# The update of the samples' retention state moves into each head's retention

## The chip, the cores and the metric

The kernel runs on one core of a Trainium2 chip. The metric is the device time of one execution in microseconds (us). Engines in the text: PE (TensorE, matrix products; its weight loads are listed as PEld), DVE (VectorE), ACT (ScalarE), POOL (GpSimd) and SP (SyncE, which issues most loads).

## The reference, cut to what matters

One step of a one-layer decoder with a prompt group (512 tokens) and a sample group (8 sequences of 8 new tokens). The layer adds up three sub-layers: a mixer of 8 retention heads and 8 differential-attention heads, a cross-attention to memory tokens and a SwiGLU FFN, each with a norm before and after. For the samples each retention head starts from a given state, gives its output and hands back the new state. With one chunk of 8 tokens for each sample:

```
scores = jnp.einsum('bihd,bjhd->bhij', qb, kb) * intra[None]
o = jnp.einsum('bhij,bjhv->bihv', scores, vb) + jnp.einsum('bihd,bhdv->bihv', qb, s) * q_dec
s_new = s * chunk_dec + jnp.einsum('bjhd,bjhv->bhdv', kb * k_dec, vb)
```

The last line is what the change moves. It is an output of its own (`ret_sample`, in the kernel `rets`), and nothing later in the layer reads it.

## The kernel before, in words

All activations stand with features on the 128 partitions and 576 columns (512 prompt tokens, 64 sample tokens). The stages, in the order of time: the input projection; the attention stage (455 to about 992 us), a loop over 8 heads; the output projection, up to 1179 us; a first handover; the query projection with the memory tokens' norm; cross-attention and its output product w_xo, up to 1416 us; a second handover; the gate, up and down products, up to the end. A handover is a norm between two dense products: DVE or POOL adds the last squares into an accumulator (line 1059 or 1169), `bcast_rstd` (from line 173) sums it over the partitions with 12 small passes on PE (`rsb_pr`, L179), takes the root on ACT and the reciprocal on DVE, spreads the factor with products against ones (`rsb_ps`, L203) and copies it. Then `prep_b1` or `prep_b2` scale the tiles and add the residual (`ym`, L1225 and L1227, L1474 and L1218), and the first product of the next stage can start.

One turn of the attention loop does, for head h: `ret_dense` (the projections of q, k, v of the next retention head in half blocks, L118), `diff_prompt` (the differential attention of the prompt), `sample_unit` (that of one sample sequence, whose key and value pages POOL gathers, `ku` and `vu`), `ret_head` (the retention) and `ret_gate`. `ret_head` puts the samples' keys (scaled by the decay) and values into a small tile `kvs` (`kns` and `vns`, lines 884 to 888). Further down it loads the samples' state in two groups of four samples into a tile `s0` of 256 KB (L951, on SP's queue) and multiplies it by the queries (`ros`, L952 and L962). `s0` has one buffer, so the second group's load waits until the first group's products have read it; the trace calls it `s`.

The update of the state is not in that loop. `ret_head` stores `kvs` to a scratch in DRAM (`kvd`, L889). In the two handovers `load_kvs` (L1102) loads it back, two heads at a time, and `state_update` runs sixteen times, eight in each handover: it loads a group's state again (L1107), forms `vbd`, the values spread over four blocks with the other samples' rows at zero (`bdm` is a mask of 0 and 1; L1108, DVE), multiplies it by the keys (`ru`, L1114, PE, a float32 product in two passes of 512 columns), does `s0 = s0 * decay + ru` (L1115, DVE) and stores the result to `rets` (L1116, on ACT's queue). `filler` places three updates ahead of the norm, three inside it behind the request for the bank of `rsb_pr`, and two after it.

What sets the order: the program is written in this order, and a planner that simulates the engines' time orders each engine's instructions and gives out the buffers. On the chip every engine, and every queue of transfers' issues, works in the order that the planner fixed. PSUM has eight banks; in attention three of them have the tag "a" (`bank_a`: scores, transposes and results of `diff_prompt`), one is that of `ret_head` (`rbank`). The pools of the next stage take over the banks and the SBUF of a closed one, and wait for its last reader. `r512` is a tag of three buffers of 128 x 512, used by `ret_head`.

Of the kernel before, what the change touches and what calls it, by code (L numbers as in the profile page):

```python
# [48 lines left out]
def step_kernel(ctx: ExitStack, tc: tile.TileContext, a: dict, o: dict):  # L49
# [164 lines left out]
    def slot(i, name, dtype=F32):  # L214
        pool = ap_ if i < 32 else spool["s2"]
        return pool.tile([P, T], dtype, tag=SL[i], name=name)
# [10 lines left out]
    def opslot(op, st):  # L227
        return op * 8 + st
# [129 lines left out]
    with ExitStack() as pha:  # L358
# [3 lines left out]
        gd = dp.tile([8, P, T], F32, name="gd")  # L362
        rawd = dp.tile([7, P, T], F32, name="rawd")
        kdec = cA.tile([P, 16], F32, name="kdec")
        kvd = dp.tile([NS, 8, 2 * P], F32, name="kvd")
        ph1 = pha.enter_context(ExitStack())
        spool["s2"] = ph1.enter_context(tc.tile_pool(name="s2a", bufs=1))
        fa = ph1.enter_context(tc.tile_pool(name="fa", bufs=1))
# [133 lines left out]
        def bank_a(name):  # L502
            return paa.tile([P, 512], F32, tag="a", name=name)
# [30 lines left out]
        def r512(name):  # L534
            return tA.tile([P, 512], F32, tag="r512", name=name, bufs=3)

        def rsmall(name, w=2):
            return tA.tile([P, 8], F32, tag="smallr", name=name, bufs=2)[:, :w]
# [165 lines left out]
        def sample_unit(b):  # L704
# [117 lines left out]
            if b == NB - 1:  # L822
                for h in range(8):
                    S.dma_start(mixd[8 + h][:, TP:], msb[:, h, :])

        NGA = 5
        omd = dp.tile([7 - NGA, P, T], F32, name="omd")
        rot = [None, None]
# [40 lines left out]
        def ret_head(h, q, k, v):  # L869
# [16 lines left out]
            kns, vns = kvs[:, :P], kvs[:, P:]  # L886
            V.tensor_scalar(kns, pss[:NS, 0:P], kdec[:NS, 8 + h : 9 + h], None, ALU.mult)
            V.tensor_copy(vns, pss[:NS, P : 2 * P])
            S.dma_start(kvd[:, h, :], kvs)  # L889
            V.tensor_tensor(  # L890
                scz[:, :, 24:32],
                pss[:NS, 256:320].rearrange("p (b t) -> p b t", b=NB),
# [55 lines left out]
            for g in range(2):  # L948
                pg = pos[:, g * P : (g + 1) * P]
                s0 = tA.tile([P, 4, P], F32, tag="s0", name=f"s0_{h}_{g}", bufs=1)  # L950
                SY.dma_start(s0, a["state"][h][:, 4 * g : 4 * g + 4, :])  # L951
                TE.matmul(  # L952
                    pg,
                    scz[:, 4 * g : 4 * g + 4, :].rearrange("p b c -> p (b c)"),
                    vns,
                    start=True,
                    stop=False,
                    skip_group_check=True,
                )
                for j in range(4):  # L960
                    c0 = TP + 8 * (4 * g + j) - 24
                    TE.matmul(  # L962
                        pg[32 * j : 32 * j + 32],
                        qd[:, c0 : c0 + 32],
                        s0[:, j, :],
                        start=False,
                        stop=True,
                        skip_group_check=True,
                    )
            rs = rsmall(f"rs{h}", 2)  # L970
            for g in range(2):
                sq = tA.tile([P, P], F32, tag="ssqr", name=f"rsqs{h}_{g}", bufs=1)
# [121 lines left out]
            t = kept[k]  # L1094
        xr.append(t)

    bdm = cp.tile([NS, NB], F32, name="bdm")
    SY.dma_start(bdm, a["bdm"])

    def load_kvs(i, sl):  # L1100
        t = slot(sl, f"kvs{i}_{sl}")[:NS, :512].rearrange("p (h c) -> p h c", h=2)
        SY.dma_start(t, kvd[:, 2 * i : 2 * i + 2, :])  # L1102
        return t

    def state_update(i, s0, vbd, kv, pu):
        h, c = i // 2, i % 2
        SY.dma_start(s0, a["state"][h][:, 4 * c : 4 * c + 4, :].rearrange("p b v -> p (b v)"))  # L1107
        V.tensor_tensor(  # L1108
            vbd.rearrange("p (b v) -> p b v", b=4),
            kv[:, h % 2 : h % 2 + 1, P:].to_broadcast([NS, 4, P]),  # L1110
            bdm[:, 4 * c : 4 * c + 4].unsqueeze(2).to_broadcast([NS, 4, P]),
            ALU.mult,
        )
        TE.matmul(pu, kv[:, h % 2, :P], vbd, start=True, stop=True)  # L1114
        V.scalar_tensor_tensor(s0, s0, (1.0 - 2.0 ** (-5.0 - h)) ** 8, pu, ALU.mult, ALU.add)  # L1115
        S.dma_start(o["rets"][h][:, 4 * c : 4 * c + 4, :].rearrange("p b v -> p (b v)"), s0)  # L1116

    NBF = 8
    sui = iter(range(16))

    def filler(kvs, s0l, vbl, bk):
        def fill(n):
            for _ in range(n):
                i = next(sui)
                s0 = slot(s0l[i % len(s0l)], f"s0_{i}")[:, :512]
                vbd = slot(vbl[i % len(vbl)], f"vbd{i}")[:NS, :512]
                state_update(i, s0, vbd, kvs[i // 4], bk(f"ru{i}"))

        def wrapped(n):
            def f(name):  # L1130
                t = bk(name)
                if name.endswith("_pr"):
                    fill(n)
                return t

            return f

        return fill, wrapped

    fill, wrapped = filler(  # L1140
        {i: load_kvs(i, opslot(OBL, i)) for i in range(NBF // 4)},
        [opslot(OBL, st) for st in (2, 3, 4, 5)],
        [opslot(OBL, st) for st in (6, 7)],
        fb2,
    )
    fill(3)
    bcast_rstd(acc1, rsb, D, T, "rsb1", wrapped(3))
    fill(2)
    ph2.close()

    pctx = ctx.enter_context(ExitStack())
# [304 lines left out]
    def fbank(name):  # L1456
        return pf.tile([P, 512], F32, tag="f", name=name)

    fill, wrapped = filler(
        {i: load_kvs(i, opslot(OAH, 1 + i - NBF // 4)) for i in range(NBF // 4, 4)},  # L1460
        [opslot(OAL, st) for st in range(1, 6)],
        [opslot(OAH, 3), opslot(OAL, 0)],
        fbank,
    )
    fill(3)
    bcast_rstd(acc3, rsf, D, T, "rsb2", wrapped(3))
    fill(2)

    e2 = strassen_env(fp, fbank)

# [471 lines left out]
```

## Time and profile before

| | us |
|---|---|
| median of 3 runs (lowest, highest) | 2993.5 (2993.02, 2995.7) |
| profiled execution, span of its instructions | 2994.0 |
| PE busy in it | 2856.2 (95%) |
| DVE, ACT, POOL busy | 2244.7, 1325.6, 369.1 |

The profile is of one execution. It gives no separate time for the profiled execution beside its span; that span lies among the times of the three runs. "Busy" is the share of the span in which an engine had an instruction; matmuls are pipelined and their ends are modelled. A row of a timeline gives start, duration, engine, line and operation, the output and the inputs by tile name, how many instructions are merged, and in square brackets the engine's idle time before it with what ended it.

### The profile page before, as it was taken

The page shows a single profiled execution, that of the slowest core. Times are in us where ns is not written, and L with a number is a line of the kernel's source. Part 1 is how long each engine was busy: PE and PEld are TensorE (multiplying, and loading weights), DVE is VectorE, ACT ScalarE, POOL GpSimd, SP SyncE. Part 2 cuts the span into 40 slices and gives each one's busy share as a digit, 9 for nine tenths or more (in the row PEclk, how much of TensorE's full clock was granted, in tenths as well). Part 3 has the DMA queues.
Part 4 walks back from the last instruction along what each step waited for, and adds up shares of the span by engine and source line. Part 5 has one row for each costly group of instructions (what it writes and reads, how often), then busy time and mean ns, then how long its engine had stood idle before and what let it go on. Part 6 is the DMA issues. An engine that isn't in the chain of part 4 may idle for free.

```text
span 2994.0 us, 54633 instructions
## 1 busy us (share of the span) xinstructions
PE 2856.2 (95%) x22060; PEld 2728.2 (91%) x22060; DVE 2244.7 (75%) x3464; ACT 1325.6 (44%) x2177; POOL 369.1 (12%) x340
## 2 busy tenths in 40 slices
PE   7899999999999999799799999999999999999996
PEld 7899998887877998788699999999999999999995
DVE  8677777555555876853798888888887877888986
ACT  7333344443445653544554444444444435433441
POOL 4000003323232021603500000000000000000004
PEclk9999999999999999899799999999999999999998
DMA  4433336666665445853734444444444465465431
GB/s 164 140 120 127 120 126 229 233 211 227 225 207 177 160 135 203 237 181 120 190 113 148 151 125 154 145 131 150 140 134 146 141 234 201 176 210 207 173 120 64
DMA packets 205336, 493.63 MB, mean 165 GB/s; under 512 B 26099, under 2 KB 68083, under 8 KB 205084
## 3 DMA queue, kind: packets, MB, share of 16 engines
q1 hardware_dynamic: 123420, 334.14, 34.5%
q0 software_dynamic: 22464, 75.38, 8.1%
q10 hardware_dynamic: 59200, 80.63, 7.4%
q8 instruction: 173, 2.83, 0.4%
q14 instruction: 79, 0.65, 0.1%
HBM read 407.08 MB, written 85.61 MB: 165 GB/s over the span
## 4 chain that ended last, share of the span: by engine, by line
PE 76%; DMA 7%; DVE 7%; issue 6%; ACT 2%; POOL 1%; SPq 1%; DVEq 0%; ACTq 0%; POOLq 0%
PE dX L1648 8%; PE Yg L307 6%; PE Yu L307 6%; PE Yin L307 5%; PE Xg L307 4%; PE dZ L1648 4%; PE Zu L307 4%; PE Zg L307 4%; PE Xu L307 4%; PE Xin L307 3%; PE Zin L307 3%; PE dY L1648 2%; PE Ywo L307 2%; PE rk L118 2%; PE xo L118 2%
## 5 line engine op out<-in xcount | busy, mean ns | idle before, releaser
L1648 PE MATMUL dX<-fo,wd 128*128 128x288 f32 x1872 | 269.4, 295 | 2.5 <-ACT ysl L54 2.5
L1648 PEld LDWEIGHTS dX<-fo,wd 128*128 128x128 f32 x1872 | 255.6, 188 | 2.8 <-ACT ysl L54 2.8
L1768 POOL TENSOR_TENSOR fin<-fin,ysq 128x320 f32<-128x320 f32 (+1 forms) x10 | 8.4, 841 | 1444.4 <-ACT ysq L54 1444.4
L54 ACT ACTIVATE wd<-wr_d 128x512 fp32r<-128x512 f32 x156 | 97.7, 630 | 119.8 <-PE dX L1648 56.7
L1648 PE MATMUL dZ<-fo,wd 128*128 128x288 f32 x936 | 139.4, 295 | 0.0
L1648 PEld LDWEIGHTS dZ<-fo,wd 128*128 128x128 f32 x936 | 129.2, 188 | 0.3 <-ACT ysl L54 0.3
L106 DVE TENSOR_TENSOR wd<-wr_d,wd 128x512 fp32r<-128x512 f32 x156 | 106.4, 687 | 12.4 <-ACT wd L54 11.6
L695 POOL DMA_INDIRECT vu<-cv,idx x64 | 61.6, 963 | 168.5 <-PE ou L787 124.2
L54 ACT ACTIVATE wd<-d 128x512 fp32r<-128x512 f32 x78 | 48.9, 631 | 75.6 <-PE dZ L1648 40.4
L1648 PE MATMUL dY<-fo,wd 128*128 128x288 f32 x468 | 75.5, 295 | 0.0
L695 POOL DMA_INDIRECT ku<-ck,idx x64 | 63.5, 993 | 94.9 <-PE su L726 57.6
L307 PE MATMUL Xg<-op,wh_p1g 128*128 128x288 f32 x336 | 67.6, 296 | 0.0
L307 PE MATMUL Xu<-op,wh_p1u 128*128 128x288 f32 x336 | 67.6, 296 | 0.0
L1648 PEld LDWEIGHTS dY<-fo,wd 128*128 128x128 f32 x468 | 66.7, 188 | 0.0
L54 ACT ACT_TABLE_LOAD x45 | 57.7, 1283 | 18.0 <-PE rsb_pr L179 11.9
L328 DVE TENSOR_TENSOR w_s1g<-w_a21g,wr_a22g 128x1024 f32<-128x1024 f32 x21 | 25.7, 1225 | 48.3 <-DMA w_a21g<-w_gate 48.3
L106 DVE TENSOR_TENSOR wd<-d,wd 128x512 fp32r<-128x512 f32 x78 | 53.5, 689 | 9.8 <-ACT wd L54 9.2
L307 PEld LDWEIGHTS Xg<-op,wh_p1g 128*128 128x128 f32 x336 | 53.9, 188 | 0.0
L307 PEld LDWEIGHTS Xu<-op,wh_p1u 128*128 128x128 f32 x336 | 53.9, 188 | 0.0
L307 PE MATMUL Xin<-op,wh_p1in 128*128 128x288 f32 x256 | 51.7, 296 | 0.0
L307 PE MATMUL Yg<-oph,wh_p7g 128*128 128x288 f32 x168 | 50.2, 299 | 1.1 <-DVE u2g L333 1.1
L307 PE MATMUL Yu<-oph,wh_p4u 128*128 128x288 f32 x168 | 49.7, 296 | 1.5 <-DVE u3u L347 1.5
(1153 smaller groups left out, 11132.2 us busy)
## 6 DMA issues: line engine op xcount, KB each, us to landing
fo<-fo SPq DMA_DIRECT2D x140, 288.0 KB
wr_d<-w_down SPq DMA_DIRECT2D x39, 512.0 KB
d<-w_down SPq DMA_DIRECT2D x39, 512.0 KB
fo<-sh ACTq DMA_DIRECT2D x60, 288.0 KB
fo<-sl ACTq DMA_DIRECT2D x60, 288.0 KB
w_a21g<-w_gate SPq DMA_DIRECT2D x21, 512.0 KB
wr_a11g<-w_gate SPq DMA_DIRECT2D x21, 512.0 KB
wr_a22g<-w_gate SPq DMA_DIRECT2D x21, 512.0 KB
```

Of the source, the lines that this page charges most:

```text
L54: S.activation(out, in_, func, **kw)
L106: V.tensor_tensor(lo, src, hi.bitcast(F32), ALU.subtract)
L118: TE.matmul(po, ws, x[h][xi], start=start and i == 0, stop=stop and i == 2)
L307: TE.matmul(bk[:, :HN], w[wx][:, st, :], ops[op][st][xi], start=first and st == 0 and i == 0, stop=st == 7 and i == 2, skip_group_check=True,)
L328: V.tensor_tensor(s1, a21, a22, ALU.add)
L695: G.indirect_dma_start(t, None, src, bass.IndirectOffsetOnAxis(ap=idx[:, pg : pg + 1], axis=0))
L1648: TE.matmul(bk[:, :HN], w[wi][:, st, :], ops[e][st][xi], start=start and st == 0 and i == 0, stop=st == 3 and i == 2, skip_group_check=True,)
L1768: (V if j % 2 == 0 or j > 11 else G).tensor_tensor(ac[:, hs], ac[:, hs], sq, ALU.add)
```

## The change

The update moves into the loop over the groups in `ret_head`, behind the products that read the state. There it uses the `s0` that is loaded already and the keys and values that are still in `kvs`. `vbd` takes a buffer of `r512`, the product takes a bank of `bank_a`, the result goes into `s0` itself and from there to `rets`. The scratch `kvd`, its stores and loads, the second load of the state, `state_update`, `filler` and the slots that they used go away. The mask is loaded once, in the attention stage. The two calls of `bcast_rstd` take plain banks.

```diff
-            S.dma_start(kvd[:, h, :], kvs)
...
+        bdm = cA.tile([NS, NB], F32, name="bdm")
+        SY.dma_start(bdm, a["bdm"])
...
                 (in ret_head, for g in range(2), after the products of s0)
+                vbd = r512(f"vbd{h}_{g}")[:NS]
+                V.tensor_tensor(
+                    vbd.rearrange("p (b v) -> p b v", b=4),
+                    vns.unsqueeze(1).to_broadcast([NS, 4, P]),
+                    bdm[:, 4 * g : 4 * g + 4].unsqueeze(2).to_broadcast([NS, 4, P]),
+                    ALU.mult,
+                )
+                pu = bank_a(f"ru{h}_{g}")
+                TE.matmul(pu, kns, vbd, start=True, stop=True)
+                s0f = s0.rearrange("p b v -> p (b v)")
+                V.scalar_tensor_tensor(s0f, s0f, g8, pu, ALU.mult, ALU.add)
+                S.dma_start(o["rets"][h][:, 4 * g : 4 * g + 4, :], s0)
...
-    fill, wrapped = filler(
-        {i: load_kvs(i, opslot(OBL, i)) for i in range(NBF // 4)},
-        [opslot(OBL, st) for st in (2, 3, 4, 5)],
-        [opslot(OBL, st) for st in (6, 7)],
-        fb2,
-    )
-    fill(3)
-    bcast_rstd(acc1, rsb, D, T, "rsb1", wrapped(3))
-    fill(2)
+    bcast_rstd(acc1, rsb, D, T, "rsb1", fb2)
...
-    fill(3)
-    bcast_rstd(acc3, rsf, D, T, "rsb2", wrapped(3))
-    fill(2)
+    bcast_rstd(acc3, rsf, D, T, "rsb2", fbank)
```

## Rows read from the trace of the kernel before

**Rows 1.** The page's first part: each engine's busy time, share, instructions.
```profile
PE 2856.2 (95%) x22060; PEld 2728.2 (91%) x22060; DVE 2244.7 (75%) x3464; ACT 1325.6 (44%) x2177; POOL 369.1 (12%) x340
```
**Rows 2.** Windows: stretch, length, busy PE PEld DVE ACT POOL, clock, DMA share, GB/s.
```profile
1178.90:1200.70 21.80, 15.94 (x34) 6.74 (x33) 15.58 (x25) 7.09 (x13) 2.02 (x3) 0.61 0.90 325
1416.10:1441.30 25.20, 17.76 (x34) 7.14 (x33) 16.81 (x26) 6.39 (x11) 1.11 (x2) 0.57 0.50 154
...
455.00:992.00 537.00, 509.51 (x4742) 427.67 (x4740) 303.95 (x836) 241.96 (x597) 167.21 (x175) 0.98 0.62 211
```
**Rows 3.** Windows of 4 us in the handovers, the same columns.
```profile
1180.00:1184.00 4.00, 3.05 (x7) 0.65 (x5) 2.54 (x3) 3.92 (x6) 1.43 (x2) 0.98 0.92 324
...
1196.00:1200.00 4.00, 2.92 (x4) 0.67 (x2) 3.72 (x7) 1.35 (x3) 0.00 (x0) 0.50 0.58 203
...
1436.00:1440.00 4.00, 2.58 (x4) 0.49 (x2) 4.00 (x7) 1.13 (x2) 0.88 (x1) 0.50 0.17 66
```
**Rows 4.** Timeline of the first handover.
```profile
1178.91 3.02 PE L1114 MATMUL ru<-vbd,kvs 64*128 64x512 f32 x6
...
1180.61 1.40 POOL L1059 TENSOR_TENSOR acc<-acc,osq 128x576 f32<-128x576 f32 x1 [0.59 <-ACT osq L54]
...
1183.78 0.69 DVE L1115 SCALAR_TENSOR_TENSOR s<-s,ru 128x512 f32<-128x512 f32 x1 [1.22 <-DMA s<-state]
1184.38 0.75 DVE L1059 TENSOR_TENSOR acc<-acc,osq 128x576 f32<-128x576 f32 x1
...
1189.49 2.08 PE L179 MATMUL rsb_pr<-ones,acc 128*96 128x1 f32 x12
...
1197.25 0.69 DVE L1115 SCALAR_TENSOR_TENSOR s<-s,ru 128x512 f32<-128x512 f32 x1 [0.28 <-PE ru L1114]
...
1198.64 0.78 ACT L54 ACTIVATE h2h<-ym,gains 128x576 fp32r<-128x576 f32 x1 [3.94 <-DVE ym L1227]
...
1199.87 0.68 DVE L1115 SCALAR_TENSOR_TENSOR s<-s,ru 128x512 f32<-128x512 f32 x1
...
1200.69 1.30 PE L118 MATMUL xq<-h2h,wh_xq 128*128 128x288 f32 x4 [1.77 <-ACT mt L54]
```
**Rows 5.** Timeline of the second handover.
```profile
1418.11 0.75 DVE L1169 TENSOR_TENSOR acc<-acc,psq 128x576 f32<-128x576 f32 x1
...
1427.81 2.08 PE L179 MATMUL rsb_pr<-ones,acc 128*96 128x1 f32 x12
...
1437.49 0.68 DVE L1115 SCALAR_TENSOR_TENSOR s<-s,ru 128x512 f32<-128x512 f32 x1
1438.08 1.42 DVE L1218 TENSOR_TENSOR ym<-ym,xk 128x576 f32<-128x576 f32 x2
...
1441.27 0.61 PE L118 MATMUL gu0a<-op,wh_gu 128*128 128x288 f32 x1 [2.69 <-ACT op L54]
```
**Rows 6.** The update's tiles: durations in ns (lowest/median/highest), first and last start.
```profile
L1114 PE MATMUL ru<-vbd,kvs x32: 589/1054/1219, 1178.9 to 1437.5; 64*128 64x512 f32 x32
L1108 DVE TENSOR_TENSOR vbd<-kvs,bdm x16: 676/677/1632, 1176.6 to 1428.5; 64x512 f32<-64x512 f32 x16
...
L1115 DVE SCALAR_TENSOR_TENSOR s<-s,ru x16: 672/687/689, 1183.8 to 1439.4; 128x512 f32<-128x512 f32 x16
```
**Rows 7.** Chain of waits, attention and first handover: start, us, what.
```profile
649.79 4.64 DMA s<-state
...
1187.56 4.05 DMA o_rets<-s
```
**Rows 8.** Waits of PE and of SP's queue, attention stage: total us, times, longest.
```profile
PE ros L962 <- DMA s<-state: 1.7, 2, 1.1
...
SPq L951 <- PE ros L962: 43.5, 9, 16.6
```
**Rows 9.** Timeline of the query stage, DVE and POOL.
```profile
1249.67 12.37 DVE L109 SCALAR_TENSOR_TENSOR mhl<-mt,gains,mhl 128x256 fp32r<-128x256 f32 x1 [0.25 <-ACT mhl L54]
...
1259.41 0.99 POOL L1190 TENSOR_TENSOR macc<-macc,mt 128x256 f32<-128x256 f32 x1
```

More of the change, by code (lines that the diff above doesn't have):

```diff
@@ L364, in step_kernel @@
         kdec = cA.tile([P, 16], F32, name="kdec")
-        kvd = dp.tile([NS, 8, 2 * P], F32, name="kvd")
         ph1 = pha.enter_context(ExitStack())
@@ L1095, in step_kernel @@
         xr.append(t)
[L1097 to L1112, printed above, removed]
-        )
[L1114 to L1138, printed above, removed]
-    fill, wrapped = filler(
-        {i: load_kvs(i, opslot(OBL, i)) for i in range(NBF // 4)},
-        [opslot(OBL, st) for st in (2, 3, 4, 5)],
-        [opslot(OBL, st) for st in (6, 7)],
-        fb2,
-    )
-    fill(3)
-    bcast_rstd(acc1, rsb, D, T, "rsb1", wrapped(3))
-    fill(2)
+    bcast_rstd(acc1, rsb, D, T, "rsb1", fb2)
     ph2.close()
@@ L1457, in fbank @@
         return pf.tile([P, 512], F32, tag="f", name=name)
[L1459 to L1464, printed above, removed]
-    fill(3)
-    bcast_rstd(acc3, rsf, D, T, "rsb2", wrapped(3))
-    fill(2)
+    bcast_rstd(acc3, rsf, D, T, "rsb2", fbank)
     e2 = strassen_env(fp, fbank)
```

## Prediction

> **What bounds the kernel now.** I read the page's engine shares first: TensorE is busy for 95% of the span, and no other engine comes near [rows 1]. A mean over stages does not price a move between two stages, so the next view is the table of windows over the three stretches that the change touches [rows 2]: the attention stage (455 to 992 us), the handover from the output projection to the query projection (1178.9 to 1200.7) and the one from w_xo to the gate and up product (1416.1 to 1441.3). In the attention stage PE is busy for 509.5 of 537 us at a granted clock of 0.98, DVE for 304, POOL for 167: PE is the bound, with 27.5 us of gaps. In the handovers PE shows 15.9 of 21.8 us and 17.8 of 25.2 us, but the dense work stands still and the clock is about 0.6. What runs there is the update and two short products of the norm. The timeline of both [rows 4, 5] shows which of it the next stage waits for; the grouped view of the update's tiles [rows 6] prices it; the chain and the waits around the loads of the state [rows 7, 8] show what the update meets in attention.
>
> **What the handovers give back.** In the first one the sum of squares is finished by DVE's add at 1184.38. Its other operand was ready when POOL's add ended, at 1180.61 + 1.40 = 1182.0. DVE stood behind an update (1183.78) that waited for its state to land. Without updates the add ends at 1182.0 + 0.75 = 1182.8. The norm's column sums on PE started only at 1189.49, behind update products in PE's queue; now they can start at about 1182.9, which is 6.6 us earlier [rows 4]. From there to the first query product three more updates of s0 lie in DVE's queue. Two of them (one is at 1197.25) stand ahead of the first normalised tile: some 0.6 us each, 1.2. The first xq product (1200.69) starts 0.14 us after the third ends (1199.87 + 0.68 = 1200.55), although its operand was ready at 1198.64 + 0.78 = 1199.4: the PSUM banks of the closing pool are still being read. That is 1.2 more. First handover: 6.6 + 1.2 + 1.2 = 9.0 us.
>
> In the second one the last add ends at 1418.11 + 0.75 = 1418.9 and the column sums start at 1427.81, behind six updates: 8.9 us. One update (1437.49) sits ahead of the add at 1438.08 on DVE, which feeds the first gate product at 1441.27: 0.5. Together 9.4 us [rows 5]. The sum of both is 18.4 us. What is late next is the norm's own chain (sums, square root, broadcast, scaling), which stays as it is. The clock costs nothing extra: it had fallen to 0.50 of full speed in both handovers with the updates in them, and is 0.50 in the last slice before the dense work is back [rows 3], so the sums keep their 2.08 us. The first stretch also loses 8 loads and 8 stores of 256 KB, 4.2 MB, where the queues ran at 325 GB/s [rows 2]: 12.9 us of transfer, more than the 9.0 us by which the work moves forward, so the loads should not hold it back.
>
> **What attention pays.** Each head gets two updates: two multiplies (vbd), two float32 products (ru, two passes each), two updates of s0 on DVE and two stores on ACT's queue. It loses one store to kvd; the 4 kvd loads and 16 second loads of the state go from the later stages, as attention has the state in SBUF anyway. SP gets no new load there except the small mask, once.
>
> PE: three ru products, six passes, took 3.02 us [rows 4] while the clock was at 0.98 of full [rows 3], 1.0 us each; the median pass of 1.05 us [rows 6] is at half clock. 16 x 1.0 = 16 us, in the stage that PE bounds. Bounds: 8 us if half of it falls into the 27.5 us of gaps, 16 if none does. I take 16: most gaps are waits of PE's queue for a particular operand, and nothing can overtake there.
>
> DVE: 16 x (0.68 + 0.69) = 22 us [rows 6] on an engine that is busy for 304 of 537. Cover: its idle 233 us. It is in the softmax chains' queue too; I take 1 us (0 to 22).
>
> The buffer: s0 has one slot. Today the second load of a head waits only for the first group's ros products. In the new order it waits for the update of s0 (0.69) and for its store to land, 4.05 in the nearest row [rows 7]: 4.7 us later, for 8 heads. The first load of the next head waits likewise but has most of a head (some 60 us) to spare. In SP's queue the waiting load stands in front of weight loads of the half blocks and of the q, k, v and bias loads; SP already stands 43.5 us in that place [rows 8], and the weights have three slots, so a few more us there hardly reach PE. On ACT each store waits in order behind its DVE update; the exponentials and copies of the softmax queue behind it. The ru result holds one of the three "a" banks of PSUM until its state has landed, and diff_prompt takes its banks from the same three. From below: nothing, if half-block products fill the extra time as they mostly do now, 1.7 us of PE idle for that load in the whole stage [rows 8]. From above: 8 x 4.7 = 38 us. The nearest row is the 1.7 us in two waits, 0.9 us each, under a load of 4.64 us; the new round trip is twice as long. I take one such wait for each head, 8 us with ACT's and PSUM's share in it. Attention: 16 + 1 + 8 = 25 us.
>
> After the last head the output projection needs the PSUM banks and the SBUF of the stage. Gate blocks run on PE up to about 992 and cover a round trip of 9.4 us that starts near 969. I take 0.
>
> **Sum.** -18.4 + 25 = +6.6 us on the profiled execution, whose span is 2994.0 us; the runs' median is 2993.5 us, so the span may stand for the time. Forecast: 3000 us.
>
> The first handover's add and a vbd show one more thing: the 16 multiplies have a median of 677 ns and a longest of 1632 ns [rows 6], and POOL's add was running from 1180.61 to 1182.0. In attention POOL is busy for 31% of the stage [rows 2], in the handovers for 9 and 4%. If each vbd that meets a POOL instruction takes 1.63 instead of 0.68 us, that is 16 x 0.31 x 0.95 = 4.7 us more on DVE. The Trainium skill has a rule for it ("SBUF — State Buffer", section "Who interferes with whom"): VectorE with two SBUF inputs and GpSimd shut each other out of a shared pair of ports for a whole instruction. By that rule the page gathers that POOL starts would wait as well; the longest vbd agrees with it, the median does not contradict it.
>
> **Rivals.** (1) Faster. Two things could give some 10 us more. The updates' products may fall into PE's gaps and the round trip may be covered wholly: attention +8, total -10, 2984 us. Or the query stage gains more than its start: its PE stands idle around 1250 to 1262 behind a single DVE instruction of 12.37 us, during a run of POOL adds [rows 9]. The memory tiles take the slots that the updates leave, so half of POOL's 16 memory adds, about 1 us each, can move into the empty handover: -8 on top, 2992; both together 2976. For it: PE's small wait for the state. Against it: a PE queue that is nearly full.
> (2) Slower by more: the round trip through s0 is exposed. The place is the second group's ros, the price up to 4.7 us a head. It decides once PE has no half-block products placed between the two groups. At half exposure 19 instead of 8 us: +17.6, 3012; at full exposure 3030. For it: this load is on the chain of waits already at 649.79 [rows 7]. Against it: only two waits of PE now.
> (3) DVE and POOL shut each other out as above, with the gathers late by as much: +4.7 on the forecast, 3005. For it: one slow vbd. Against it: PE waits for DVE rarely in that stage.
> (4) The change doesn't do what it says: the handovers don't shorten, because another wait takes the place of PE's queue. With half of the 18.4 us back: +15.8, 3010. Against it: both sums were ready long before PE began.
>
> **How the numbers follow.** Chances: forecast 0.45, (1) 0.25, (2) 0.15, (3) 0.10, (4) 0.05. The forecast alone reaches from 2993 to 3007. The range takes (1) down to 2982 and (2) at half exposure with a few us more, up to 3016. This kernel's measurement tells about 0.2%, 6 us, from no change, so slower begins at 2999.5 and faster at 2987.5. Half of the forecast, all of (2) and (4) and most of (3) lie above: 0.49. Most of (1) lies below: 0.20. Between: 0.31.
>
> **What would show it.** Right: the column sums start 3 to 4 us after the last dense product in both handovers, and the stretches shrink from 21.8 and 25.2 us to about 13 and 16; ru passes of 0.4 to 0.5 us stand in attention, which is about 25 us longer; PE's waits there for s grow from 1.7 us to about 8. Wrong: attention longer by under 12 us, or by over 35; a first handover that is no shorter; or a query stage that loses or gains more than its start, above all at the long DVE instruction.

## The result: 37 us slower, and the loss is in attention

The changed kernel takes 3030.4 us (median of 4 runs, 3029.27 to 3032.37); the kernel before, run beside it, 2993.7 us (4 runs, 2993.02 to 2995.7). The ratio is 1.0117, 95% interval [1.0103, 1.0132]. The forecast was 3000 us in a range of 2982 to 3016: the time lies above the range.

The page of the profile after, its first part. The span is 3029.3 us, 35.3 more than before. PE is busy for 3.9 us more [rows 1], so 31 of the 35 us are idle time of PE:
```profile
PE 2860.1 (94%) x22060; PEld 2737.5 (90%) x22060; DVE 2240.4 (74%) x3464; ACT 1330.7 (44%) x2180; POOL 375.1 (12%) x340
```
Windows of the changed kernel over the attention stage and the two handovers, columns as in [rows 2]. The handover windows reach from the last dense product to the next stage's first:
```profile
455.00:1045.00 590.00, 539.63 (x4776) 443.18 (x4774) 319.32 (x871) 250.93 (x604) 169.70 (x175) 0.95 0.58 200
1232.75:1245.50 12.75, 4.37 (x17) 3.17 (x16) 5.39 (x9) 7.04 (x17) 7.67 (x9) 0.60 0.64 233
1458.60:1474.40 15.80, 4.35 (x17) 3.18 (x17) 8.52 (x14) 6.35 (x11) 1.70 (x2) 0.56 0.29 93
```
Against [rows 2] the attention stage is 53 us longer (590 for 537), the first handover 9.0 us shorter (12.8 for 21.8) and the second 9.4 (15.8 for 25.2). Both handovers shrank by what was forecast. The timeline of the changed kernel shows how (compare [rows 4, 5]):
```profile
1232.46 0.29 PE L307 MATMUL Zwo<-oph,wl_p3wo 128*128 128x288 f32 x1
...
1235.56 0.76 DVE L1071 TENSOR_TENSOR acc<-acc,osq 128x576 f32<-128x576 f32 x1 [2.31 <-POOL acc L1071]
1236.37 2.08 PE L179 MATMUL rsb_pr<-ones,acc 128*96 128x1 f32 x12 [3.62 <-DVE acc L1071]
...
1245.51 1.33 PE L118 MATMUL xq<-h2h,wh_xq 128*128 128x288 f32 x4 [3.40 <-ACT h2h L54]
...
1458.14 0.42 PE L118 MATMUL xo<-oh,wl_xo 128*128 128x288 f32 x2
1461.53 2.05 PE L179 MATMUL rsb_pr<-ones,acc 128*96 128x1 f32 x12 [2.97 <-ACT yx L54]
...
1474.39 0.61 PE L118 MATMUL gu0a<-op,wh_gu 128*128 128x288 f32 x1 [5.81 <-ACT op L54]
```
The column sums now start 3.6 and 3.0 us after the last dense product; before, they started 10.5 and 11.7 us after it. So the account, from the first and last dense products of the stages in both traces, is: attention +53.3, output projection +0.5, first handover -9.0, query and cross-attention stage -2.4, second handover -9.3, the rest +2.2. The sum is +35.3, which is the difference of the spans.

Now the attention stage. The timeline of the changed kernel, retention of head 0 from the first group's products (`ros`) to the first transpose of head 1 (`rkn`); below it the end of head 6:
```profile
488.90 0.65 PE L962 MATMUL ros<-s,qd 128*32 128x128 f32 x8
...
524.08 0.66 PE L617 MATMUL nt_d<-ident,on 128*128 128x128 f32 x4
...
526.53 1.98 PE L978 MATMUL ru<-vbd,kvs 64*128 64x512 f32 x4
528.73 0.69 DVE L980 SCALAR_TENSOR_TENSOR s<-s,ru 128x512 f32<-128x512 f32 x1 [4.68 <-PE ru L978]
...
529.45 0.34 ACTq L981 DMA_DIRECT2D o_rets<-s  x1
...
536.38 0.33 SPq L951 DMA_DIRECT2D s<-state  x1
...
545.52 0.43 PE L962 MATMUL ros<-s,qd 128*32 128x128 f32 x8
...
551.50 0.38 PE L997 MATMUL rot<-ident,rob 128*128 128x128 f32 x2
...
558.03 1.11 PE L877 MATMUL rkn<-ident,rk 128*128 128x128 f32 x4
...
980.49 0.38 PE L997 MATMUL rot<-ident,rob 128*128 128x128 f32 x2
...
983.72 0.60 PE L877 MATMUL rkn<-ident,rk 128*128 128x128 f32 x4
```
The same place in the kernel before:
```profile
495.43 0.43 PE L962 MATMUL ros<-s,qd 128*32 128x128 f32 x8
...
504.69 0.40 PE L962 MATMUL ros<-s,qd 128*32 128x128 f32 x8
...
516.87 0.39 PE L985 MATMUL rot<-ident,rob 128*128 128x128 f32 x2
...
528.02 0.66 PE L876 MATMUL rkn<-ident,rk 128*128 128x128 f32 x4
```
Three things are to be seen. The two `ros` of head 0 are 56.6 us apart and not 9.3. Head 0 is the extreme: in the other seven they are 8 to 27 us apart, and were 4 to 9 before. The largest piece in head 0 is 38 us in which the first group's update waits: `ru` comes at 526.53, behind `nt_d`, the last transpose of the prompt's attention of the same head. In all eight heads it starts within 2 us of the end of that transpose. In six of the other heads it stands 2 to 17 us behind the end of `ros`, in head 5 ahead of it; with head 0 these waits add up to 97 us. From `ru` to the second `ros` it takes 19 us in head 0 and 9 to 12 in the others. And at the end of the head the next one's `rkn` follows `rot` by 6.5 us, later by 3.2, where before it had 11.2. All retention products but `ru` use one PSUM bank (`rbank`), so the retentions of the eight heads form one chain: `rkn` to the first `ros` (front), first to second `ros` (between), second `ros` to `rot` (back), `rot` to the next `rkn` (gap). The smallest gaps are 2 to 3 us; I read them as a next head that takes the bank as soon as it is free, and a longer gap as a wait for something else, its q, k, v. Sums over the eight heads, worked out from those rows of the timelines (first `rkn` at 465 to 467 everywhere):

| kernel | between | back | front | gap | last `rot` | first product of the next stage |
|---|---|---|---|---|---|---|
| before | 55 | 61 | 344 | 60 | 986 | 992 |
| changed | 188 | 43 | 318 | 29 | 1044 | 1045 |
| e1, no update | 62 | 54 | 336 | 62 | 979 | 988 |
| e13, no product | 92 | 49 | 316 | 53 | 976 | 990 |
| e3, two buffers | 8 | 68 | 350 | 82 | 975 | 1004 |
| e6, two buffers, `ru` in the bank of `ros` | 87 | 94 | 314 | 46 | 1007 | 1011 |
| e10, own result | 175 | 42 | 292 | 33 | 1008 | 1010 |
| e7, no store | 167 | 49 | 296 | 36 | 1015 | 1016 |
| e9, load on POOL | 177 | 51 | 302 | 26 | 1022 | 1025 |
| e8, scratch only | 192 | 45 | 301 | 35 | 1038 | 1044 |
| e5, `ru` in the bank of `ros` | 145 | 99 | 307 | 27 | 1045 | 1046 |
| e4, two buffers, `ru` in d | 6 | 56 | 310 | 180 | 1017 | 1051 |
| e2, `ru` in d | 94 | 62 | 287 | 139 | 1048 | 1073 |

In the changed kernel between and back are 115 us longer than before. The gaps took up 31 of it, front is 26 shorter, and the chain ends 58 us later. The next stage starts right behind its last `rot`, first the changed kernel, then before:
```profile
1044.36 0.66 PE L997 MATMUL rot<-ident,rob 128*128 128x128 f32 x2 [6.29 <-DVE rob L989]
1045.43 0.61 PE L118 MATMUL wo0a<-op,wh_wo 128*128 128x288 f32 x1 [0.40 <-ACT rom L54]
```
```profile
985.77 0.38 PE L985 MATMUL rot<-ident,rob 128*128 128x128 f32 x2
...
992.16 0.40 PE L118 MATMUL wo0a<-op,wh_wo 128*128 128x288 f32 x1 [1.50 <-ACT op L54]
```
So in the changed kernel the end of the chain sets the end of the stage. How much the chain can take before that happens is not the sum of its gaps alone: in e6 and e10 between and back are 65 and 101 us longer than before, the gaps took up 14 and 27 us of it and front 30 and 52. A caution for all windows of single executions: with the same code there, the attention stage ended at 992 us before and at 984 and 981 in e12 and e11, so differences of some 10 us in one stage are not read as effects.

### The profile page after: what moved, and what is told of

Same layout as the page of the kernel before. It is cut to its first block, busy times and chain, and to the rows that moved or that the text cites. A ratio compares the mean times of both kernels' runs of the same rounds, so it can differ in the third digit from the quotient of the medians.

```text
span 3029.3 us, 54593 instructions
## 1 busy us (share of the span) xinstructions
PE 2860.1 (94%) x22060; PEld 2737.5 (90%) x22060; DVE 2240.4 (74%) x3464; ACT 1330.7 (44%) x2180; POOL 375.1 (12%) x340
## 4 chain that ended last, share of the span: by engine, by line
PE 70%; issue 5%; DVE 4%; DMA 3%; ACT 1%; POOL 1%; ACTq 0%; DVEq 0%; POOLq 0%; SPq 0%
PE dX L1601 8%; PE Yu L307 7%; PE Yg L307 6%; PE Zu L307 4%; PE Xu L307 4%; PE Zg L307 4%; PE Xg L307 4%; PE dZ L1601 4%; PE rk L118 3%; PE dY L1601 2%; PE Ywo L307 2%; PE rv L118 2%; PE xo L118 2%; PE mem L118 2%; PE rg L118 2%
## 5 line engine op out<-in xcount | busy, mean ns | idle before, releaser
L106 DVE TENSOR_TENSOR wd<-wr_d,wd 128x512 fp32r<-128x512 f32 x156 | 106.3, 686 | 12.5 <-ACT wd L54 11.8
L694 POOL DMA_INDIRECT vu<-cv,idx x64 | 62.1, 970 | 172.3 <-PE ou L786 119.0
L694 POOL DMA_INDIRECT ku<-ck,idx x64 | 65.0, 1016 | 114.9 <-PE su L725 76.9
L1071 POOL TENSOR_TENSOR acc<-acc,osq 128x576 f32<-128x576 f32 x14 | 26.0, 1858 | 210.2 <-DMA yd<-og 120.6
L307 PE MATMUL Zg<-oph,wh_p5g 128*128 128x288 f32 x168 | 49.5, 295 | 1.0 <-ACT wh_p5g L54 1.0
```

What stands on the lines that cost most here:

```text
L106: V.tensor_tensor(lo, src, hi.bitcast(F32), ALU.subtract)
L307: TE.matmul(bk[:, :HN], w[wx][:, st, :], ops[op][st][xi], start=first and st == 0 and i == 0, stop=st == 7 and i == 2, skip_group_check=True,)
L694: G.indirect_dma_start(t, None, src, bass.IndirectOffsetOnAxis(ap=idx[:, pg : pg + 1], axis=0))
L1071: (V if j == KT - 1 else G).tensor_tensor(acc1, acc1, sq, ALU.add)
```

## The experiments

Times are medians; ratios are to the kernel before, run beside each. Windows rows have the columns of [rows 2].

**e1, no update at all.**
```diff
-    (from before) load_kvs, state_update, filler, every fill(n), kvd and its stores
+    bcast_rstd(acc1, rsb, D, T, "rsb1", fb2)
+    bcast_rstd(acc3, rsf, D, T, "rsb2", fbank)
```


> The kernel before with the update of the samples' state left out altogether (the new state is not written; everything else stays), and both handovers hold the norm alone. It prices the handovers by themselves: attention keeps its length of 537 us to within a few us, since only the eight small stores of the keys and values leave it. Theory (the handovers give back what was forecast, 18.4 us, and all of the loss is in attention): 2975 us, between 2971 and 2979. Rival (the handovers do not shorten for want of the update; another wait takes its place): 2985 to 2993 us. Against the changed kernel this run is 55 us shorter by the theory, and that would be the full price of the update inside attention.

Measured: 2969.3 us, ratio 0.9944 [0.9924, 0.9963], attention 533 us. By the medians the update cost 20 us in the handovers, by the ratio 17: the forecast of 18.4 lies between (the interval of the ratio is 11 to 23 us). The median lies 2 us under the expected 2971 to 2979, in a series in which the kernel before took 2989.1 us. In the profile the handovers are 13.3 and 15.7 us long. The theory holds, and attention is where the loss is.
```profile
455.00:988.00 533.00, 510.29 (x4743) 429.00 (x4741) 301.07 (x835) 238.40 (x594) 168.11 (x175) 0.98 0.62 213
```
**e2, the product in a bank of the half blocks.**
```diff
-                pu = bank_a(f"ru{h}_{g}")
+                pu = pda.tile([P, 512], F32, tag="d", name=f"ru{h}_{g}")
```


> The changed kernel with one word different: the update's product ru takes a PSUM bank of the three of the half blocks (tag d) and not one of the three of the prompt's attention (tag a). Theory A (ru waits for an a bank and then holds it over the wait for DVE, so that two chains block each other): most of the loss beyond PE's own 16 us goes, 3000 to 3010 us, and the time from the first group's last product to ru falls from a mean of some 14 us to under 5. Theory B (the round trip through the one buffer of s0, that is update, store and next load): ru comes earlier but the second group's load still waits for the store, 3020 to 3030 us. Theory C (it is only PE's work for ru and no wait): 3030 us unchanged.

Measured: 3062.1 us, ratio 1.0243 [1.0221, 1.0265]. None of the three expected it. `ru` does come early, and the distance of the groups falls to a mean of 11.8 us; but the gap grows to 139 us: `rkn` now comes 10 to 36 us behind `rot`. The next head's q, k, v come from the half blocks whose banks `ru` now shares; that this is what `rkn` waits for is argued from the code, not shown. A mean distance of 11.8 with a worse time also says that the distance is not what sets the time by itself.

**e3, two buffers for s0.**
```diff
-                s0 = tA.tile([P, 4, P], F32, tag="s0", name=f"s0_{h}_{g}", bufs=1)
+                s0 = tA.tile([P, 4, P], F32, tag="s0", name=f"s0_{h}_{g}", bufs=2)
-                jk = tA.tile([P, P], F32, tag="ssq", ...)     (and ssq2, ssqr)
-                act(jk, po[:, :P], AF.Square, accum_out=...)
+                act(at[:, :P], po[:, :P], AF.Square, accum_out=...)
```


> The changed kernel with two buffers for s0; to make room, three scratch tiles for squares that nobody reads go, and the squares are written into tiles that are overwritten or dead afterwards. Both groups' loads can start at once, and the second group's products no longer wait for the first group's update and store. Theory A (PSUM banks): the second group's products come soon after the first, but ru still waits for and holds an a bank: 3010 to 3025 us. Theory B (round trip through s0): the distance between the two groups falls from a mean of 23.5 us to under 5, and the time to 2990 to 3000 us, what is left being PE's 16 us less the 18.4 of the handovers. Theory C (PE's work alone): 3030 us unchanged.

Measured: 2989.8 us, ratio 1.0007 [0.9992, 1.0021]. As theory B expected, at its lower edge; the distance of the groups is 1.0 us. The first head and the stage in the trace:
```profile
491.49 0.43 PE L959 MATMUL ros<-s,qd 128*32 128x128 f32 x8
...
492.54 0.65 PE L959 MATMUL ros<-s,qd 128*32 128x128 f32 x8
...
503.26 0.44 PE L993 MATMUL rot<-ident,rob 128*128 128x128 f32 x2
...
526.74 1.98 PE L975 MATMUL ru<-vbd,kvs 64*128 64x512 f32 x4
```
```profile
455.00:1004.00 549.00, 523.00 (x4781) 431.69 (x4779) 331.43 (x874) 249.94 (x607) 169.34 (x175) 0.98 0.62 215
```
`ru` is as late as in the changed kernel (526.7), but no `ros` and no `rot` waits for it. 41 of the 53 us are gone. What is left above e1 is 16 us of stage (19 us by the ratios), which agrees with the price of PE's products that the prediction had, as far as single executions can tell.

**e4, both.** The two edits above at once.

> Both of the former at once: two buffers for s0, and ru in a bank of the half blocks. Theory A or B: 2990 to 3000 us, that is before minus 18.4 for the handovers plus at most 16 for PE's products and some rest; if both are part of the cause it lies below each of the two single edits. Theory C (PE's work and the order, no wait): 3020 to 3030 us.

Measured: 3032.8 us, ratio 1.0145 [1.0124, 1.0166]. All theories missed. With the state there early, `ru` runs ahead of `ros` and then holds its bank until the update behind `ros` has read it, over 16 us here:
```profile
569.72 1.12 PE L975 MATMUL ru<-vbd,kvs 64*128 64x512 f32 x2
...
571.16 1.12 PE L975 MATMUL ru<-vbd,kvs 64*128 64x512 f32 x2
...
587.05 0.49 PE L949 MATMUL ros<-kvs,scz 64*128 64x128 f32 x2
```
The chain's gaps are 180 us, 18 to 41 from each head to the next (139 in e2).

**e5, the product in the bank of ros, one buffer.**
```diff
-                pu = bank_a(f"ru{h}_{g}")
-                TE.matmul(pu, kns, vbd, start=True, stop=True)
-                V.scalar_tensor_tensor(s0f, s0f, g8, pu, ALU.mult, ALU.add)
+                pu = pos[:, 256:512]
+                for c in (slice(0, 256), slice(256, 512)):
+                    TE.matmul(pu, kns, vbd[:, c], ..., skip_group_check=True)
+                    V.scalar_tensor_tensor(s0f[:, c], s0f[:, c], g8, pu, ...)
```


> The changed kernel, one buffer for s0, with the update's product in columns 256 to 511 of the bank that the products ros already hold (they use columns 0 to 255), in two halves with an update of s0 after each. No bank of the tag a is asked for. Theory (banks of a tag are given out in the order of the program, where ru stands behind the whole of the head's prompt attention, so ru comes only after that chain's last transpose nt_d, and with one buffer of s0 the second group waits for it): the distance of the two groups falls from a mean of 23.5 us to 10 to 13 us, what update, store and load take by themselves, and the time to 2998 to 3012 us. Rival (the store and the next load are the cost, wherever ru stands): the time stays at 3020 to 3030 us.

Measured: 3032.6 us, ratio 1.0122 [1.0091, 1.0153]: no gain. That misses the theory, and lies 3 us above the range of the rival. The distance fell to 18.1 and not to 10 to 13, and back rose by 56 us, as the halves wait in turn for DVE:
```profile
577.02 0.43 PE L962 MATMUL ros<-s,qd 128*32 128x128 f32 x8
577.37 0.70 PE L980 MATMUL ros<-vbd,kvs 64*128 64x256 f32 x2
...
581.85 0.70 PE L980 MATMUL ros<-vbd,kvs 64*128 64x256 f32 x2
...
595.09 0.43 PE L962 MATMUL ros<-s,qd 128*32 128x128 f32 x8 [1.94 <-DMA s<-state]
```
Between and back together are 244 us, no shorter than in the changed kernel (231). So the wait for the prompt's bank is the largest piece of head 0, yet taking it away in this form only put other waits into the same chain. What a bank without such a wait would give with one buffer stays open.

**e6, two buffers and the bank of ros.** The edits of e3 and e5.

> The kernel with two buffers for s0, and the update's product in columns 256 to 511 of the bank of ros, in two halves. With two buffers the second group waits for nothing anyway; ru now comes right behind ros and leaves the prompt's banks alone, but the four halves and updates, some 5 us, lie in the retention's chain. Theory (with two buffers only PE's work for ru is left): 2985 to 2993 us, as with the banks of the prompt. Rival (the prompt's banks still cost something with two buffers): below 2985 us. Rival (the longer chain of the retention costs): above 2995 us.

Measured: 2992.8 us, ratio 1.0008 [0.9996, 1.0021]. As the theory expected: e3 and e6 agree, though between and back are 181 us in e6 and 76 in e3. So with two buffers neither the prompt's banks nor a longer chain costs anything that can be measured.

**e7, no store of the new state; e10, the update into a tile of its own.**
```diff
e7  -                S.dma_start(o["rets"][h][:, 4 * g : 4 * g + 4, :], s0)
e10 +                sn = tA.tile([P, 4, P], F32, tag="sn", ..., bufs=1)   (room as in e3)
e10 +                V.scalar_tensor_tensor(sn..., s0f, g8, pu, ALU.mult, ALU.add)
e10 +                S.dma_start(o["rets"][h][:, 4 * g : 4 * g + 4, :], sn)
```


> The changed kernel without the stores of the new state, so that the new state does not leave the chip; s0 is free as soon as the update on DVE has read and written it. It splits the round trip. Theory (the wait of ru for the prompt's banks makes most of it): 3010 to 3025 us, 8 times the 4 to 5 us of a store's landing less at most. Rival (the store's landing is what the second load waits for): 2990 to 3000 us, as with two buffers.

> The changed kernel, one buffer for s0, in which the update on DVE writes into a tile of its own (one buffer, in the room of the three scratch tiles for squares) and the store leaves from there. The state's next load waits for the update on DVE only, not for the store to land; the stores and their bytes stay. Theory (the wait for the landing is the price): as without stores, 2996 to 3006 us, SP's wait for s0 near 28 us and not 70.8. Rival (the stores' bytes or their place in ACT's queue are the price): 3020 to 3030 us.

Measured: e7 3001.8 us, ratio 1.0030 [1.0016, 1.0044]; e10 2998.2 us, ratio 1.0032 [1.0018, 1.0046]. First e7, then e10:
```profile
455.00:1015.00 560.00, 527.96 (x4774) 434.83 (x4772) 321.30 (x871) 255.43 (x607) 168.80 (x175) 0.97 0.59 203
```
```profile
455.00:1009.00 554.00, 522.67 (x4777) 429.11 (x4775) 318.37 (x868) 244.02 (x599) 168.78 (x175) 0.99 0.62 211
```
By the ratios 26 and 25 us of the changed kernel's 35 are gone. e7 did not do what its theory expected (3010 to 3025), and lies 2 us above the range of its rival: the wait for the landing is worth more than the theory had. e10, as its theory expected by the time, shows that most of it is the wait and not the stored bytes, which are all there; part of its gain may come from the scratch tiles (e8). Its other sign missed: SP's queue waits 50.3 us for `s0`, not near 28 as in e7. And the sum of between and back fell only by 14 us in both; the other part of their gain is in front (22 and 26 us).

**e8, the scratch tiles alone.** e3's edit without the second buffer.

> The changed kernel with one buffer for s0 and the three scratch tiles for squares gone, the squares written where the kernel with two buffers writes them. Theory (the second buffer made the difference, the scratch tiles nothing): 3026 to 3034 us. Rival (the removed scratch tiles freed the squares from waits): 3000 us or less.

Measured: 3020.9 us, ratio 1.0088 [1.0064, 1.0112], under the expected 3026; the attention stage keeps its 589 us. By the ratios it is 9 us faster than the changed kernel, though the two intervals overlap. Against e8, e3 gains 24 us and e10 17, so the larger part of both gains is not the scratch tiles'.

**e9, the state's loads on POOL's queue.**
```diff
-                SY.dma_start(s0, a["state"][h][:, 4 * g : 4 * g + 4, :])
+                G.dma_start(s0, a["state"][h][:, 4 * g : 4 * g + 4, :])
```


> The changed kernel, one buffer for s0, with one thing different: the loads of the state are issued from POOL's queue and not from SP's. The round trip through s0 stays as long as it is; what changes is who stands behind the waiting load. In the changed kernel SP's queue waits 70.8 us in 13 times for the store of s0 to land, with the loads of weights and of q, k, v behind it. Theory (the price is that wait at the head of SP's queue: the dense blocks get their weights late, so nothing fills the retention's wait): 2995 to 3012 us, with the gathers of key and value pages behind POOL's wait as the reason for the rest. Rival (the price is the retention's own longer chain, wherever the load waits): 3022 to 3032 us.

Measured: 3004.4 us, ratio 1.0053 [1.0032, 1.0074], as the theory of SP's queue expected. Between and back stay at 228 us; front is 16 shorter.

**e13, the round trip without the product.**
```diff
-                V.tensor_tensor(vbd..., vns..., bdm..., ALU.mult)
-                TE.matmul(pu, kns, vbd, start=True, stop=True)
-                V.scalar_tensor_tensor(s0f, s0f, g8, pu, ALU.mult, ALU.add)
+                V.tensor_scalar(s0f, s0f, g8, None, ALU.mult)
```


> The changed kernel, one buffer for s0, with the mask product on DVE and the product ru on PE left out: the state is only multiplied by its decay in place and stored, so the state that comes out lacks the new keys and values. The round trip through s0 (a DVE pass behind the first group's products, the store, the next load) stays, and PE has no work for the update. Theory (the round trip with SP's queue behind it is one cost, PE's products another): the round trip alone 2995 to 3012 us, that is 25 to 40 us above the kernel without any update (2969), and SP's wait for the store's landing stays above 50 us. Rival (the loss comes only where products, their bank and the round trip meet): 2970 to 2982 us.

Measured: 2973.4 us, ratio 0.9956 [0.9939, 0.9972], in the range of the rival. The theory that e9 had seemed to show falls. Waits of SP's queue in the attention stage (total, times, longest), first in the changed kernel, then in e13:
```profile
SPq L951 <- DMA o_rets<-s: 70.8, 13, 16.9
```
```profile
SPq L951 <- DMA o_rets<-s: 67.8, 12, 14.9
```
The windows row of e13:
```profile
455.00:990.00 535.00, 507.65 (x4744) 425.25 (x4742) 311.40 (x854) 250.55 (x605) 170.56 (x175) 0.98 0.63 220
```
The state's loads stand at the head of SP's queue about as long as in the changed kernel, and the stage is as long as without any update (535 and 533 us). So neither the update, store and load by themselves nor SP's wait cost much. Between is 92 us here and the chain keeps 53 us of gaps. The DVE pass of the first group starts 0.1 to 4.2 us behind the end of `ros` in the eight heads; in the changed kernel, where it needs the product, 0.4 to 39.2 us. So the loss comes only with the product in the round trip. e13 takes out the mask product, `ru` and its bank at once and does not tell them apart.

**e11 and e12, the updates left in the handovers, in another order.**
```diff
e11 -    fill(3)
e11 -    bcast_rstd(acc1, rsb, D, T, "rsb1", wrapped(3))
e11 -    fill(2)
e11 +    bcast_rstd(acc1, rsb, D, T, "rsb1", fb2)
e11 +    fill(8)
...
e12 +    fill(3)                (loads, vbd and ru only)
e12 +    bcast_rstd(acc1, rsb, D, T, "rsb1", wrapped(1))   (at rsb_ps, not rsb_pr)
e12 +    finish()               (updates of s0 and stores so far)
e12 +    fill(4)
e12 +    finish()
```


> The kernel before, its sixteen updates in the handovers as they were, but all eight of a handover written behind the norm instead of three ahead, three inside and two behind. The column sums no longer queue behind the updates' products; these stand behind the broadcast and ahead of the next stage's first product, and from the third on each waits for a mask product of DVE between the scalings of the tiles. Theory (what a handover costs is where the updates stand, and behind the broadcast they delay the first product): 2985 to 2995 us, no gain. Rival (the sums were all that mattered): 2975 to 2983 us.

> The kernel before with its sixteen updates in the handovers, the one that stood inside the norm ahead of the sums moved: three products ahead of the column sums, one between the sums and the broadcast, four behind it, and each update of s0 on DVE written behind the norm. Theory (PE idles in the norm's chain for some 9 us of each handover, and products that fill only that are free): 2978 to 2988 us. Rival (DVE's updates and the four products ahead of the next stage delay it as before): 2988 to 2996 us.

Measured: e11 2988.2 us, ratio 1.0004 [0.9989, 1.0019]; e12 2983.4 us, ratio 0.9970 [0.9954, 0.9986]. e12 beats both kernels, by 0.3% of before. Its first handover:
```profile
1173.01 0.29 PE L307 MATMUL Zwo<-oph,wl_p3wo 128*128 128x288 f32 x1
...
1179.87 2.08 PE L179 MATMUL rsb_pr<-ones,acc 128*96 128x1 f32 x12 [3.62 <-DVE acc L1059]
...
1192.29 2.07 PE L1114 MATMUL ru<-vbd,kvs 64*128 64x512 f32 x2 [0.60 <-DVE vbd L1108]
...
1198.20 0.82 PE L118 MATMUL xq<-h2h,wh_xq 128*128 128x288 f32 x2 [3.84 <-DVE s L1119]
```
The sums come early, 6.6 us after the last dense product, but the last updates still stand ahead of the next stage, and this handover is 24.9 us long, 3 more than before. The second takes 21.2 us and not 25.2. Together that is 1 us, so the time came in as the theory expected, but its mechanism, idle PE time in the norm's chain, is not seen in the handovers. In its profile the stage from the first query product to the last of w_xo is 8 us shorter (207 for 215), and attention, whose code is the same, 8 us, which is what executions differ by. Where e12's gain of 0.3% comes from is not shown. e11 warns of reading a handover's length as its price: its two last 39.2 and 39.7 us, 32 us more than before, and its time is the same. In its profile the stage from the first query product to the last of w_xo is 18 us shorter than before (198 for 215), and what follows the second handover 12 us.

## Why the prediction was wrong, by its own steps

- **Handovers, -9.0 and -9.4: right.** Measured as 9.0 and 9.4 from the last dense product to the next. The parts fit too: up to the column sums 6.9 and 8.8 us (forecast 6.6 and 8.9), behind them 2.1 and 0.6 (forecast 2.4 and 0.5). e1 confirms the sum. The query stage gained 2.4 us beyond its start, less than the 8 that rival 1 had for it; the idle time of PE that this rival pointed at is 9.6 us in the trace before (1253.6 to 1263.2), not 12.
- **PE's products, 16 us: right.** Two updates take 1.98 us in the trace, sixteen 15.8; e3 differs from e1 by 16 us of stage, within some 10 us, so the gaps seem to have hidden little of them.
- **DVE, 1 us: not seen apart.** e13 has DVE's sixteen passes over s0, but not the sixteen multiplies, and its stage is within 2 us of e1's.
- **The buffer, 8 us: this step failed.** The prediction took "one such wait for each head", with an upper bound of 4.7 us a head for update and landing, and let half-block products fill the rest. Between and back grew by 14.4 us a head (115 over eight), and two buffers gave 41 us of stage back (e3). Two things were missed. The sum starts the round trip right behind `ros`, with no wait for the product. In the changed kernel the product is late, behind `nt_d`, as `ru` is written behind the whole of `diff_prompt` and takes its turn in the same three banks behind it; these waits are 97 us over the eight heads. Behind `ru` the round trip is near what was forecast: 9 to 12 us in seven heads, for 9.4. The prediction named the shared bank and put "PSUM's share" into the 8 us, without a wait for it. And the price was read from PE's recorded waits for that load, 1.7 us before, which were to grow to about 8. In the changed kernel there are none: the planner placed the second `ros` behind other work, and the wait shows in the retention's chain, whose end the next stage then waited for. That the late product and the wait for the landing are both needed for most of the loss is shown (e13 and e3, e7, e10); that the bank's turn alone would cost it is not, since e2 and e5, which take `ru` out of those banks, brought other waits.
- **The tail, 0: wrong in kind.** The prediction asked what covers one round trip at the end. But the chain arrives late as a whole: in the changed kernel the stage's last step is `rot` at 1044.36, and the next stage starts at 1045.43. Before, the last `rot` came 6 us ahead of the next stage.
- **Rival 2** named the right place (the second group's `ros`), and its full exposure, 3030 us, is the measured time. That match is chance, as its price was wrong: 4.7 us a head fully exposed stood in for 14.4 us a head, of which a third showed (the 37 us of the stage's 53 that are not PE's 16). Rival 3's stretched multiplies are refuted by the vbd rows below, rival 1 by the time, rival 4 by the handovers' rows and e1. "Attention longer by over 35" was the sign set for being wrong, and it came.

What stays open is the division within the 41 us. The pieces overlap: removing the wait for the landing (e7, e10) or moving the load off SP's queue (e9) gives 20 to 36 us of stage, and most of that lies in front, which no run took apart; the planner fixes another order for each kernel, and its share isn't known.

## What to carry to other kernels

Before work is moved into a loop, list the chains of that loop that go round one buffer or one bank, and add up their gaps over the turns: a first estimate of what the move may lengthen them by. Here it was no exact bound, as other parts of the chain shrank too. The bound engine's waits for that buffer did not show the cost at all. A buffer that was only read and is now written and stored is to get a second one, or a result tile of its own, as part of the same change: here that gave back 33 and 25 us by the ratios, with the share of the scratch tiles in both. Even so the move did not pay: with two buffers (e3) the time is that of the kernel before, as the products cost in attention what the handovers gave back. And a tile that an independent chain requests from a shared rotation comes when the program's order says so, not when its operands are ready.

## What the runs showed of the hardware

DVE beside POOL. Vbd and its neighbours in the changed kernel's attention stage, durations in ns (lowest/median/highest), with POOL busy for 170 of 590 us there:
```profile
L971 DVE TENSOR_TENSOR vbd<-kvs,bdm x16: 671/674/682, 486.5 to 1009.1; 64x512 f32<-64x512 f32 x16
...
L978 PE MATMUL ru<-vbd,kvs x32: 589/589/694, 526.5 to 1029.8; 64*128 64x512 f32 x32
L980 DVE SCALAR_TENSOR_TENSOR s<-s,ru x16: 675/686/690, 528.7 to 1037.7; 128x512 f32<-128x512 f32 x16
```
Not one of sixteen was stretched. Seven of them overlapped an instruction of POOL that issues a gather of pages; none met an add. It is the gather that took longer: the two that began while a multiply ran took 1.23 and 1.37 us, the 40 that overlapped no DVE instruction 0.93 to 0.97. One of the two:
```profile
593.62 0.67 DVE L971 TENSOR_TENSOR vbd<-kvs,bdm 64x512 f32<-64x512 f32 x1
...
593.87 1.23 POOL L694 DMA_INDIRECT ku<-ck,idx  x1 [3.37 <-PE ou L786]
```
In e11's second handover the same multiply, started 0.17 us ahead of an add on POOL, took 2.48 us:
```profile
1423.51 2.48 DVE L1108 TENSOR_TENSOR vbd<-kvs,bdm 64x512 f32<-64x512 f32 x1
...
1423.68 1.74 POOL L1480 TENSOR_TENSOR acc<-acc,yx 128x576 f32<-128x576 f32 x1
```
In all eight cases in which this multiply was stretched (seven in e11, one before) it ended 0.55 to 0.56 us after the end of POOL's add. Three quarters of POOL's busy time in attention (62.1 and 65.0 of 169.7 us) are the instructions that issue the gathers. The Trainium skill ("SBUF — State Buffer", section "Who interferes with whom") has a shared pair of ports for which DVE with two SBUF inputs contends with a GpSimd instruction that reads SBUF. The rows of e11 agree with it. The rows in attention show that POOL's busy share can't be multiplied by the price of an add, as the prediction's rival did.

The clock. Where PE had more idle time in the attention stage, the granted clock, a mean over stretches at full and at half speed, was lower: 0.95 in the changed kernel with 50 us of idle time and 0.92 in e2 and e4 with 54 and 41, against 0.98 before with 27.5. PE was busy for 30 us more there than before, of which its 32 new passes are 15.8.
